# Two transformer stacks on one core: the plain blocks of the feed-forward's up projection go over to seven products, and attention scores are made two heads at a time

## The chip, the cores and the metric

The kernel runs on one core of a Trainium2 chip. TensorE (PE in the profile) multiplies matrices; VectorE (DVE) and ScalarE (ACT) work element by element; GpSimd (POOL) and SyncE (SP) mostly issue transfers. Each engine takes its instructions in the order in which the program lists them. The metric is the device time of one execution, 3244.63 us as the median of three runs (3244.62 to 3246.77). All arithmetic that matters is in single precision.

## The reference

512 tokens of width 1024 pass through four layers, each a mixer and then a feed-forward part, both added to x. Layers 1 and 2 mix with an mLSTM, an RG-LRU and a sparse attention (8 heads of width 64); their feed-forward has 3072 hidden columns. Layers 3 and 4 mix with a full attention and a memory attention; their feed-forward has 2816. What the change touches:

```
def rms_norm(x, g):
    return x * lax.rsqrt(jnp.mean(x * x, -1, keepdims=True) + EPS) * g

# feed-forward, layers 1 and 2
h = rms_norm(x, norm_ffn[l])
ff_g, ff_u = jnp.split(h @ ffn_up[l], 2, axis=-1)
ff_g = causal_dwconv(ff_g, ffn_conv_w[l], ffn_conv_b[l])
x = x + (jax.nn.gelu(ff_g) * ff_u) @ ffn_down[l]
# layers 3 and 4: x + (silu(gate) * up) @ w_down, without a convolution

# sparse attention, for each of 8 heads of width 64
att = einsum('bqhd,bqkhd->bqhk', q, k_sel) * Dh ** -0.5
p = softmax(where(keep, att, -inf)); y = einsum('bqhk,bqkhd->bqhd', p, v_sel)
```

The factor rsqrt(...) belongs to a token alone, so it may be applied to h @ W as well as to h.

## The kernel before

x is kept transposed, as eight tiles of 128 columns of the width by 512 tokens. A single-precision product is made of three products in a faster format (`three`, L436): every weight and every activation is split into a high and a low half, the high one by ACT (L361) and the low one by DVE (L369). So a weight chunk costs one `wh<-raw` and one `wl<-raw,wh` of 128x1024, and a matmul of the program shows as three of the trace.

The program is not written in the order in which it runs. Parts of it are generators; a list scheduler that runs when the kernel is built (`Issue`, L98) takes from them whatever its own table of durations and the priorities say is ready, and so fixes the order on each engine. Every engine then follows that order, ready or not. Temporaries are 66 slots of 128x512 and eight banks for results of TensorE; a part that finds too few slots waits for its turn.

**Norm.** `Norm.add(c)` (L919) runs when tile c of x is final: it makes the pair `hh`, `hl` of x g, and adds the squares to `nacc`. After the eighth, `finish` (L945) sums over the width on TensorE (`ps_st`), takes the root (`rn`, on POOL) and spreads it over the partitions (`ps_bc`): R, which is 1/rms for every token.

**Up projection.** `ffn` (L1890) goes through blocks of 256 gate columns and 256 up columns. The first two (`NOLD`) are *plain*: 192 matmuls of 512 columns in all, 96 a block, that read `hh` and `hl`, so that they can start before R is known; R is applied to their results. The other blocks use seven products in place of eight (a Strassen scheme): the inputs are cut into 2x2 quarters, and sums of quarters are multiplied, P1 to P7, each 24 matmuls of 256 columns. The weights' sums are formed by accumulating transfers. The sums of the activation's quarters (`xa`, `xb`, `xs`) are made by `Seven.build` (L1752) out of x g R, once, beside the plain blocks. P1 and P2 share a bank, so do P6 and P7, P5 and P3; P4 has its own. The order is a written list: P7 of the block before comes after P1, then P2, P5, the P4 and P3 of the block before, P6. Groups of two blocks are then multiplied down (`ps_t<-ff`), in units placed between the products.

**Sparse attention.** `dsa_head` (L1550) makes the scores of one head (`ps_at`), 20 matmul records on 64 of the 128 rows of the array; then DVE masks, ACT takes the exponent, DVE divides, PE transposes (`ps_pt`), ACT copies (`pT`), PE multiplies with v (`ps_y`). A head takes 12 slots. Two heads lie in one tile of q and of k, one in rows 0 to 63, the other in rows 64 to 127.

Of the kernel before, what the change touches and what calls it, by code (L numbers as in the profile page):

```python
# [17 lines left out]
P = 128  # L18
# [8 lines left out]
NOLD = 2  # L27
# [39 lines left out]
WIDTH = 4  # L67
ORDER = ("qi small mv av swap rx0 rx2 rg0 rg2 mk0 mk4 mk2 mk6 mo0 mo2 aq b0 b2 b6 ak b4 a0 a2 a4 a6 c0 c2 c4 c6",) * 2
# [261 lines left out]
def kernel(ctx, tc, a, out):  # L330
# [217 lines left out]
    behind, later = Chain(None, 0), Chain(None, 2)  # L548

    def after(fn, chain=behind):  # L550

        old, order.cur = order.cur, chain
        fn()
        order.cur = old
# [89 lines left out]
    def proj_t(w, c0, ntile, src, evac, ready=None, pre=None, ktiles=8, need=3):  # L644

        for i0 in range(0, ntile, 2):
# [433 lines left out]
    def first_mix(l, norm, nxt):  # L1080
# [454 lines left out]
        py, npv = {}, {}  # L1535
        nd = [0]

        def dsa_all():
            while len(masks) < NT or len(st["qcT"]) < NT or len(st["kcT"]) < NT or len(av) < NT:
                yield "wait"  # L1540
            for h in range(8):
                spawn(dsa_head(h), PRIO["dsa"])
                yield
                yield
# [5 lines left out]
        def dsa_head(h):  # L1550
            qc, kc = st["qcT"], st["kcT"]
            hp = h // 2
            rg = slice(64 * (h % 2), 64 * (h % 2) + 64)
            while len(slots.left) < 12:
                yield "wait"
            pr = [slots.take(F32, "pr") for _ in range(NT)]
            mx, nm, ssum = sm(4, "mx"), sm(4, "nm"), sm(4, "ss")
            where = {}

            def score(*tbs):  # L1560
                o = 0
                ps = yield from gbank("ps_at", 1)
                for tb in tbs:
                    for sb in range(tb + 1):
                        mm32(ps.t[:, o + sb * P:o + (sb + 1) * P], qc[tb].t[rg, hp * P:(hp + 1) * P],
                             kc[sb].t[rg, hp * P:(hp + 1) * P])
                    where[tb] = (ps, o)
                    o += (tb + 1) * P

            def top(t0, *tbs):  # L1570
                for tb in tbs:
                    ps, o = where[tb]
                    S = (tb + 1) * P
                    masked(pr[tb].t[:, 0:S], ps.t[:, o:o + S], masks[tb][:, 0:S], mx[:, tb:tb + 1])
                for ps in dict.fromkeys(where[tb][0] for tb in tbs):
                    ps.free()
                vts(nm[:, t0:t0 + len(tbs)], mx[:, t0:t0 + len(tbs)], -0.125, ALU.mult)

            def expo(*tbs):
                for tb in tbs:  # L1580
                    S = (tb + 1) * P
                    act(pr[tb].t[:, 0:S], pr[tb].t[:, 0:S], AF.Exp, scale=0.125, bias=nm[:, tb:tb + 1],
                        accum_out=ssum[:, tb:tb + 1])

            def norm_(t0, *tbs):
                recip(ssum[:, t0:t0 + len(tbs)], ssum[:, t0:t0 + len(tbs)])
                for tb in tbs:
                    S = (tb + 1) * P
                    vts(pr[tb].t[:, 0:S], pr[tb].t[:, 0:S], ssum[:, tb:tb + 1], ALU.mult)

            yield from score(0, 1)
            yield from score(2)
            yield
            top(0, 0, 1, 2)
            yield from score(3)
            yield
            expo(0, 1, 2)
            top(3, 3)
            yield
            norm_(0, 0, 1, 2)  # L1600
            expo(3)
            yield
            norm_(3, 3)
            yield
            pT = {}
            for grp in (((0, 0),), ((1, 0),), ((2, 0), (3, 256))):
                ps = yield from gbank("ps_pt", 1)
                for sb, o in grp:
                    tr(ps.t[:, o:], [pr[tb].t[:, sb * P:(sb + 1) * P] for tb in range(sb, NT)])
                if grp[0][0] == 0:  # L1610
                    ps0 = ps
                    continue
                if grp[0][0] == 1:
                    ps1 = ps
                    yield
                    for sb, p_ in ((0, ps0), (1, ps1)):
                        pT[sb] = (yield from grab("pT"))[0]
                        act(pT[sb].t[:, 0:T - sb * P], p_.t[:, 0:T - sb * P])
                        p_.free()
                    continue  # L1620
                yield
                b = (yield from grab("pT"))[0]
                act(b.t[:, 0:384], ps.t[:, 0:384])
                ps.free()
            for p_ in pr:
                p_.free()
            yield
            while hp not in py:
                if len(banks.left) > 2:
                    py[hp] = banks.take(F32, "ps_y")  # L1630
                else:
                    yield "wait"
            for sb in range(NT):
                N = T - sb * P
                v = b.t[:, (0 if sb == 2 else 256):][:, 0:N] if sb >= 2 else pT[sb].t[:, 0:N]
                mm32(py[hp].t[rg, sb * P:T], av[sb].t[:, h * 64:(h + 1) * 64], v, sb == 0, sb == NT - 1)
            for p_ in (pT[0], pT[1], b):
                p_.free()
            nd[0] += 1
            npv[hp] = npv.get(hp, 0) + 1  # L1640
            if npv[hp] == 2:
                p = yield from gpair("yc")
                split2(py[hp].t, p.h, p.l)
                py[hp].free()
                yc[hp] = p
            if nd[0] == 8:
# [93 lines left out]
        yield from proj_t(a["w_out"][l], 0, 8, lambda: [merged[i] for i in range(8)], ev_o, pre=pre_o, need=4)  # L1740
# [4 lines left out]
    class Seven:  # L1745
# [3 lines left out]
        def __init__(self):  # L1749
            self.v, self.bufs, self.done = {}, [], False  # L1750

        def build(self, norm):  # L1752
            yield from until(lambda: norm.R is not None)
            for k in range(KH):
                while len(slots.left) < 10:
                    yield "wait"
                t = [slots.take(F32, "hn") for _ in range(2)]
                for j in range(2):
                    stt(t[j].t[:, 0:T], xs[k + KH * j], cc(norm.g, k + KH * j), norm.R, ALU.mult, ALU.mult)
                a11, a21 = t[0].t[:, 0:256], t[0].t[:, 256:T]  # L1760
                a12, a22 = t[1].t[:, 0:256], t[1].t[:, 256:T]
                xa = slots.take(F32R, "xa")
                xb = pair("xb")
                splits([(a11, xa.t[:, 0:256], xa.t[:, 256:T]), (t[1].t[:, 0:T], xb.h, xb.l)])
                yield
                s = [slots.take(F32, "xs") for _ in range(2)]
                s1, s2, s3, s4 = s[0].t[:, 0:256], s[0].t[:, 256:T], s[1].t[:, 0:256], s[1].t[:, 256:T]
                vtt(s1, a21, a22, ALU.subtract)
                vtt(s2, s1, a11, ALU.subtract)
                vtt(s3, a11, a21, ALU.subtract)  # L1770
                vtt(s4, a12, s2, ALU.add)
                for b in t:
                    b.free()
                yield
                ps = [pair("xs") for _ in range(2)]
                splits([(s[j].t[:, 0:T], ps[j].h, ps[j].l) for j in range(2)])
                for b in s:
                    b.free()
                self.bufs += [xa, xb] + ps
                self.v[k] = dict(A11=(xa.t[:, 0:256], xa.t[:, 256:T]))  # L1780
                for nm, p, j in (("A12", xb, 0), ("A22", xb, 1), ("S1", ps[0], 0), ("S2", ps[0], 1),
                                 ("S3", ps[1], 0), ("S4", ps[1], 1)):
                    self.v[k][nm] = (p.h[:, j * 256:(j + 1) * 256], p.l[:, j * 256:(j + 1) * 256])
                yield
            self.done = True
# [4 lines left out]

    class Block:

        def __init__(self, X, w, cols, gate, done):
            self.X, self.gate, self.done = X, gate, done
# [19 lines left out]
        BANK = dict(P1="b1", P2="b1", P6="b2", P7="b2", P4="b3", P5="b4", P3="b4")  # L1816
        NEED = dict(P1=1, P2=2, P6=1, P7=2, P4=2, P5=0, P3=4)

        def mm(self, nm, x, h, lo):
            yield from until(lambda: self.X.done and len(slots.left) >= self.NEED[nm])  # L1820
# [5 lines left out]
            for j in range(2):  # L1826
                for k in range(KH):
# [3 lines left out]
                          not first and j == 1 and k == KH - 1, skip_group_check=True)  # L1831
# [9 lines left out]
        def after_P2(self):  # L1841
            self.g = [now(name="fg") for _ in range(2)]
            for j, v in enumerate(self.halves(self.b1)):
                self.gate.first(self.g[j].t[:, 0:256], v)
            self.b1.free()

# [3 lines left out]
        def after_P6(self):  # L1850
            self.u2 = now(name="u2")
            vtt(self.u2.t[:, 0:T], self.b2.t, self.s1.t[:, 0:T], ALU.add)

# [881 lines left out]
```

## Time and profile before

| | us |
|---|---|
| median of three runs | 3244.63 |
| the profiled execution, its own time | 3243.72 |
| its span | 3241.9 |
| PE busy | 3196.7 (99%) |
| DVE busy | 2201.1 (68%) |
| ACT busy | 1574.5 (49%) |

A matmul's modelled duration overlaps the next one's, so what one costs is read from one start to the next; so for DVE and ACT, whose rows overlap a little when they are queued without a wait. `[2.41 <-ACT s L361]` behind a row says that the engine sat idle for 2.41 us before it, until that instruction released it. A matmul that the program makes in single precision without the three products (`ps_at`, `ps_sc`, `ps_st`, `ps_bc`) shows as two records.

### The profile page before, as it was taken

The numbers are of one execution on the slowest core, as the hardware profiler recorded it, in microseconds if no ns is written. First come the engines' busy times: TensorE is split into PE (matmuls) and PEld (weight loads), VectorE is DVE, ScalarE is ACT, GpSimd is POOL, SyncE is SP. The second block draws the span as 40 slices with busy tenths as digits, with TensorE's granted clock in tenths as the row PEclk, the third lists the DMA queues.
The fourth block names the chain that finished last, engine by engine and source line by source line (L and its number), as shares of the span: only waits on it lengthen the run. The fifth ranks groups of instructions, "written<-read, shape, count | busy, mean of one in ns | idle before, by whom it ended". The sixth has DMA issues, their size and how long they took to land.

```text
span 3241.9 us, 45750 instructions
## 1 busy us (share of the span) xinstructions
PE 3196.7 (99%) x17637; PEld 2713.1 (84%) x17637; DVE 2201.1 (68%) x4154; ACT 1574.5 (49%) x2694; POOL 362.0 (11%) x407
## 2 busy tenths in 40 slices
PE   8999999999999999999999999999999999999999
PEld 6778778889987778778789988878899988889998
DVE  7974544766777974544766677787766667776664
ACT  6552433444444552433444456876443457664443
POOL 2000000011110000000011112120111111101110
PEclk9999999999999999999999999999999999999999
DMA  4323223377762323123377763221577742227783
GB/s 154 99 71 91 59 71 118 98 156 173 165 155 82 98 72 91 59 71 118 98 160 172 167 158 123 65 92 48 122 177 164 183 162 66 72 72 163 163 173 94
DMA packets 350345, 380.50 MB, mean 117 GB/s; under 512 B 17519, under 2 KB 324448, under 8 KB 350128
## 3 DMA queue, kind: packets, MB, share of 16 engines
q1 hardware_dynamic: 262256, 276.47, 27.5%
q0 software_dynamic: 87840, 101.12, 18.3%
q8 instruction: 138, 2.26, 0.3%
q14 instruction: 79, 0.65, 0.1%
q10 hardware_dynamic: 32, 0.01, 0.0%
HBM read 367.05 MB, written 10.49 MB: 116 GB/s over the span
## 4 chain that ended last, share of the span: by engine, by line
PE 90%; DVE 6%; issue 2%; ACT 1%; DMA 0%; POOL 0%; SPq 0%; DVEq 0%; POOLq 0%; ACTq 0%
PE ps_t L433 46%; PE ps_u L433 21%; PE ps_n L433 11%; PE ps_at L433 2%; PE ps_y L433 2%; PE ps_pt L425 2%; DVE wl L369 1%; PE ps_at L421 1%; PE ps_y L421 1%; DVE m L1238 1%; DVE score L1239 1%; ACT pr L361 1%; PE ps_num L421 1%; DVE u L369 1%; PE ps_S L421 1%
## 5 line engine op out<-in xcount | busy, mean ns | idle before, releaser
L369 DVE TENSOR_TENSOR wl<-raw,wh 128x1024 fp32r<-128x1024 f32 (+1 forms) x647 | 774.6, 1199 | 531.9 <-ACT wh L361 526.7
L361 ACT ACTIVATE wh<-raw 128x1024 fp32r<-128x1024 f32 (+1 forms) x647 | 672.1, 1040 | 944.0 <-PE ps_t L433 422.3
L433 PE MATMUL ps_u<-xsh,wl 128*128 128x256 f32 x1216 | 341.9, 281 | 3.1 <-DVE u L369 3.1
L433 PE MATMUL ps_u<-xsh,wh 128*128 128x256 f32 x1216 | 341.5, 281 | 0.0
L433 PE MATMUL ps_u<-xsl,wh 128*128 128x256 f32 x1216 | 341.1, 281 | 0.0
L433 PE MATMUL ps_t<-ffh,wl 128*128 128x512 f32 x736 | 290.3, 396 | 5.0 <-DVE wl L369 4.9
L433 PE MATMUL ps_t<-ffl,wh 128*128 128x512 f32 x736 | 290.2, 395 | 0.7 <-DVE ffl L369 0.7
L433 PE MATMUL ps_t<-ffh,wh 128*128 128x512 f32 x736 | 290.4, 395 | 0.0
L433 PE MATMUL ps_t<-h2h,wl 128*128 128x512 f32 x704 | 283.0, 402 | 0.0
L369 DVE TENSOR_TENSOR x<-x,ps_t 128x512 f32<-128x512 f32 x232 | 159.0, 686 | 182.7 <-PE ps_t L433 182.4
L433 PE MATMUL ps_t<-h2h,wh 128*128 128x512 f32 x704 | 282.8, 402 | 0.0
L433 PE MATMUL ps_t<-h2l,wh 128*128 128x512 f32 x704 | 280.0, 398 | 0.0
L433 PEld LDWEIGHTS ps_u<-xsh,wl 128*128 128x128 f32 x1216 | 229.1, 188 | 5.7 <-DVE u L369 4.0
L433 PEld LDWEIGHTS ps_u<-xsl,wh 128*128 128x128 f32 x1216 | 228.9, 188 | 1.7
L433 PEld LDWEIGHTS ps_u<-xsh,wh 128*128 128x128 f32 x1216 | 229.0, 188 | 0.0
L433 PE MATMUL ps_u<-xbh,wl 128*128 128x256 f32 x608 | 171.4, 282 | 6.4 <-ACT s L361 6.3
L433 PE MATMUL ps_u<-xbl,wh 128*128 128x256 f32 x608 | 171.2, 282 | 0.0
L433 PE MATMUL ps_u<-xbh,wh 128*128 128x256 f32 x608 | 171.1, 281 | 0.0
L433 PEld LDWEIGHTS ps_t<-ffh,wl 128*128 128x128 f32 x736 | 138.3, 188 | 37.1 <-DVE wl L369 8.1
L416 POOL DMA_DIRECT2D raw<-in_ffn_up_dram x80 | 102.3, 1366 | 564.5 <-DVE wl L369 508.4
L433 PEld LDWEIGHTS ps_t<-ffh,wh 128*128 128x128 f32 x736 | 138.2, 188 | 32.0
L433 PEld LDWEIGHTS ps_t<-ffl,wh 128*128 128x128 f32 x736 | 138.2, 188 | 30.3 <-DVE ffl L369 1.2
(454 smaller groups left out, 7268.3 us busy)
## 6 DMA issues: line engine op xcount, KB each, us to landing
raw<-in_w_in_dram SPq DMA_DIRECT2D x128, 512.0 KB, 3.8
raw<-in_ffn_up_dram SPq DMA_DIRECT2D x96, 512.0 KB, 4.7
raw<-in_w_gate_up_dram SPq DMA_DIRECT2D x88, 512.0 KB, 3.9
raw<-in_ffn_up_dram POOLq DMA_DIRECT2D x80, 512.0 KB, 5.9
raw<-in_w_gate_up_dram POOLq DMA_DIRECT2D x72, 512.0 KB, 6.0
raw<-in_w_out_dram SPq DMA_DIRECT2D x40, 512.0 KB, 3.5
raw<-in_ffn_down_dram SPq DMA_DIRECT2D x36, 512.0 KB, 4.4
raw<-in_w_down_dram SPq DMA_DIRECT2D x32, 512.0 KB, 5.1
```

What stands on the lines that cost most here:

```text
L361: lambda: nc.scalar.activation(out=out, in_=in_, func=func, **kw),
L369: dve(0.00104, lambda: nc.vector.tensor_tensor(out=out, in0=in0, in1=in1, op=op), [out], [in0, in1])
L416: order.op("pool", 1.0, lambda: nc.gpsimd.dma_start(out=out, in_=in_, accum_op=ALU.add), [out], [out], extra=max(n, 0.05), slack=-1.0)
L421: lambda: nc.tensor.matmul(o, lhsT=lhsT, rhs=rhs, start=start, stop=stop), [o], [lhsT, rhs],
L425: order.op("pe", 0.107, lambda: nc.tensor.transpose(o, in_, idn), [o], [in_, idn], rows=in_.shape[0])
L433: lambda: nc.tensor.matmul(o, lhsT=lhsT, rhs=rhs, start=first, stop=last, **kw), [o], [lhsT, rhs],
L1238: dve(0.00104, lambda: nc.vector.max(out=m8, in_=acc), [m8], [acc])
L1239: dve(0.00104, lambda: nc.vector.match_replace(out=acc, in_to_replace=m8, in_values=acc, imm_value=MARK), [acc], [acc, m8])
```

## The change

- **Norm.** A `NormSeven` replaces the norm ahead of each feed-forward part: it makes no `hh`, `hl`, but from x g the quarters and their sums, tile by tile as x comes out of the mixer's output projection. That projection takes its tiles in the order 0 and 1, 4 and 5, 2 and 3, 6 and 7 (`TURNS`), since tiles k and k+4 are summed together.
- **Up projection.** All blocks go by seven products. R is applied to results, on DVE. P7 has a bank of its own. The first two blocks are interleaved by a written list.
- **Scores.** Heads go in pairs; the two heads' products stand alternately in the queue, in two banks; a pair takes 16 slots.

```diff
-NOLD = 2
+TURNS = (0, 4, 2, 6)
...
-        def dsa_head(h):
-            while len(slots.left) < 12:
+        def dsa_pair(hp):
+            while len(slots.left) < 16:
                 yield "wait"
...
                     for sb in range(tb + 1):
-                        mm32(ps.t[:, o + sb * P:o + (sb + 1) * P], qc[tb].t[rg, hp * P:(hp + 1) * P],
-                             kc[sb].t[rg, hp * P:(hp + 1) * P])
+                        for j, rg in enumerate(rgs):
+                            mm32(pss[j].t[:, o + sb * P:o + (sb + 1) * P], qc[tb].t[rg, hp * P:(hp + 1) * P],
+                                 kc[sb].t[rg, hp * P:(hp + 1) * P])
...
+    class NormSeven(Norm):
+        def add(self, c):
+            t = self.t[c] = now(name="xg")
+            act(t.t[:, 0:T], xs[c], scale=cc(self.g, c))
+            self.X.own(c, t)
+            k = c % KH
+            if k in self.t and k + KH in self.t:
+                spawn(self.X.sums(k, [self.t[k], self.t[k + KH]]), 0)
+            self.acc = self.sq(c, self.acc)
...
-        BANK = dict(P1="b1", P2="b1", P6="b2", P7="b2", P4="b3", P5="b4", P3="b4")
+        BANK = dict(P1="b1", P2="b1", P6="b2", P7="b7", P4="b3", P5="b4", P3="b4")
...
         def after_P2(self):
             self.g = [now(name="fg") for _ in range(2)]
+            spawn(self.first(), 0)
+
+        def first(self):
+            yield from until(self.norm.ready)
             for j, v in enumerate(self.halves(self.b1)):
-                self.gate.first(self.g[j].t[:, 0:256], v)
+                vtt(self.g[j].t[:, 0:256], v, self.norm.R[:, 0:256], ALU.mult)
...
         def gates(self):
+            R = self.norm.R
             for j in range(2):
-                self.g[j] = self.gate.rest(j, self.g[j])
+                v = self.g[j].t[:, 256:T]
+                vtt(v, v, R[:, 256:T], ALU.mult)
+            for j in range(2):
+                self.g[j] = self.gate(j, self.g[j])
+                v = self.g[j].t[:, 0:T]
+                vtt(v, v, R, ALU.mult)
...
-        for b in range(nblk):
-            if b < NOLD:
-                yield from plain(b, fs)
-                continue
...
+        for b, nm in ((0, "P1"), (0, "P2"), (1, "P1"), (1, "P2"), (0, "P5"), (0, "P7"), (1, "P5"), (0, "P6"), (1, "P7"),
+                      (0, "P3"), (1, "P6"), (0, "P4"), (2, "P1"), (1, "P3"), (2, "P2"), (1, "P4"), (2, "P5")):
+            yield B[b].u[nm]
+        yield from between(2, "P5")
```

**First place: PE at the third feed-forward part.** The queue of before, from some way into the first plain block (`hh`, `hl`: the norm's pair; `wh`, `wl`: a weight's halves):

```order
L433 MATMUL ps_t<-hh,wl 128x512
L433 MATMUL ps_t<-hl,wh 128x512
L421 MATMUL ps_st<-ones,nacc 128x1 x4
L433 MATMUL ps_t<-hh,wh 128x512
L433 MATMUL ps_t<-hh,wl 128x512
L433 MATMUL ps_t<-hl,wh 128x512
L433 MATMUL ps_t<-hh,wh 128x512
L433 MATMUL ps_t<-hh,wl 128x512
L433 MATMUL ps_t<-hl,wh 128x512
L433 MATMUL ps_t<-hh,wh 128x512
L421 MATMUL ps_bc<-ident,rn_20714 128x128 x4
```

The queue of the change at the same place, from the end of the output projection (`yoh`, `yol`) into P1 of block 0 (`ps_u<-xa`):

```order
L433 MATMUL ps_t<-yoh,wl 128x512
L433 MATMUL ps_t<-yol,wh 128x512
L433 MATMUL ps_t<-yoh,wh 128x512
L421 MATMUL ps_st<-ones,nacc 128x1 x4
L421 MATMUL ps_bc<-ident,rn_21224 128x128 x4
L433 MATMUL ps_u<-xa,wl 128x256
L433 MATMUL ps_u<-xa,wh 128x256 x2
L433 MATMUL ps_u<-xa,wl 128x256
```

Before, `ps_st` and `ps_bc` stand among plain matmuls; now they stand straight behind the projection and ahead of the first product. The fourth part has the same rows. In the first two, `ps_st` and `ps_bc` stand inside P2 of block 0.

**Second place: DVE behind P4 of block 1 in the first feed-forward part.** The queue of the change; `fg` is the gate, `fy` its convolution, R_5032 the 1/rms, `ff` what the down projection reads. In PE's queue P4 of block 1 is followed by P5 of block 2 (24 matmuls) and by the first down unit, whose first 12 matmuls read block 0's `ff` and whose next 12 read block 1's:

```order
L369 TENSOR_TENSOR fg<-fg,R_5032 128x256
L373 SCALAR_TENSOR_TENSOR fy<-fg,colt_98,fy 128x511
L373 SCALAR_TENSOR_TENSOR fy<-fg,colt_97,fy 128x510
L373 SCALAR_TENSOR_TENSOR fy<-fg,colt_98,fy 128x511
L369 TENSOR_TENSOR wl<-raw,wh 128x1024
L369 TENSOR_TENSOR fy<-fy,R_5032 128x512
L369 TENSOR_TENSOR wl<-raw,wh 128x1024
L373 SCALAR_TENSOR_TENSOR fy<-fg,colt_97,fy 128x510
L369 TENSOR_TENSOR u<-u,fy 128x512
L369 TENSOR_TENSOR fy<-fy,R_5032 128x512
L369 TENSOR_TENSOR ffl<-u,ffh 128x512
```

Ahead of these rows, since P4's end, stand three more of 128x256 and six of 128x512. Before, block 1 was plain, and its `ff` was made while P1 to P5 of block 2 ran.

**Third place: PE in the sparse attention of the first layer.** One head of before, from its transposes on (`h2h`, `h2l` and `ps_t`: another projection's matmuls):

```order
L425 MATMUL ps_pt<-ident,pr 128x128 x10
L433 MATMUL ps_t<-h2h,wl 128x512
L433 MATMUL ps_t<-h2l,wh 128x512
L433 MATMUL ps_t<-h2h,wh 128x512
L421 MATMUL ps_y<-pT,av 64x512
L421 MATMUL ps_y<-pT,av 64x384
L421 MATMUL ps_y<-pT,av 64x256
L421 MATMUL ps_y<-pT,av 64x128
L421 MATMUL ps_at<-rT 128x128 x10
```

The third pair of the change, with scores of the fourth:

```order
L425 MATMUL ps_pt<-ident,pr 128x128 x10
L421 MATMUL ps_at<-rT 128x128 x6
L421 MATMUL ps_y<-pT,av 64x512
L421 MATMUL ps_y<-pT,av 64x384
L421 MATMUL ps_y<-pT,av 64x256
L421 MATMUL ps_y<-pT,av 64x128
L421 MATMUL ps_at<-rT 128x128 x6
L425 MATMUL ps_pt<-ident,pr 128x128 x10
L421 MATMUL ps_at<-rT 128x128 x8
L421 MATMUL ps_y<-pT,av 64x512
```

Scores, transposes and products with v of two pairs now follow one another with no other projection's matmul between them, and the last pair ends shortly before its result is read; before, single heads were spread among other work, and the last ended some 220 matmuls earlier.

## Rows read from the trace of the kernel before

**Rows 1.** The page, busy time, share and instructions by engine.
```profile
PE 3196.7 (99%) x17637; PEld 2713.1 (84%) x17637; DVE 2201.1 (68%) x4154; ACT 1574.5 (49%) x2694; POOL 362.0 (11%) x407
```
**Rows 2.** The page, the chain that ended last, by engine.
```profile
PE 90%; DVE 6%; issue 2%; ACT 1%; DMA 0%; POOL 0%; SPq 0%; DVEq 0%; POOLq 0%; ACTq 0%
```
**Rows 3.** PE's waits: line, who was waited for, total us, times, longest.
```profile
PE ps_t L433 <- DVE wl L369: 7.5, 16, 1.3
PE ps_u L433 <- ACT s L361: 6.3, 4, 2.4
...
PE ps_u L433 <- DVE u L369: 3.1, 4, 0.8
```
**Rows 4.** PE's timeline, first feed-forward part's head: start, us, engine, line, operation.
```profile
597.42 0.40 PE L433 MATMUL ps_t<-hh,wl 128*128 128x512 f32 x1
...
604.11 1.05 PE L421 MATMUL ps_bc<-ident,rn 128*128 128x128 f32 x8
...
645.36 0.28 PE L433 MATMUL ps_u<-xa,wl 128*128 128x256 f32 x1
...
647.94 0.40 PE L433 MATMUL ps_u<-xa,wh 128*128 128x256 f32 x2
650.75 0.39 PE L433 MATMUL ps_u<-xbh,wl 128*128 128x256 f32 x1 [2.41 <-ACT s L361]
```
**Rows 5.** PE's timeline, third feed-forward part's head.
```profile
2270.20 0.39 PE L433 MATMUL ps_t<-hh,wl 128*128 128x512 f32 x1
...
2277.36 1.05 PE L421 MATMUL ps_bc<-ident,rn 128*128 128x128 f32 x8
...
2316.60 0.28 PE L433 MATMUL ps_u<-xa,wl 128*128 128x256 f32 x1
...
2320.36 0.39 PE L433 MATMUL ps_u<-xbh,wl 128*128 128x256 f32 x1 [0.75 <-ACT s L361]
```
**Rows 6.** Windows after the heads of parts one and two: PE busy, PEclk, DMA.
```profile
645.00:660.00 15.00, 12.59 (x84) 0.89 0.51 112
...
1617.00:1632.00 15.00, 12.59 (x90) 1.00 0.55 119
```
**Rows 7.** PE, groups of tile ps_at: instructions, ns min/median/max, first and last start.
```profile
L421 PE MATMUL ps_at<-rT x320: 272/272/373, 356.8 to 1409.4; 64*128 64x128 f32 x160
```
**Rows 8.** PE's timeline, score products on 64 rows: ps_at of one head, ps_sc.
```profile
356.79 2.50 PE L421 MATMUL ps_at<-rT 64*128 64x128 f32 x20
...
59.47 1.34 PE L421 MATMUL ps_sc<-kiT,rT 64*128 64x256 f32 x4
...
78.15 1.78 PE L421 MATMUL ps_sc<-kiT,rT 64*128 64x384 f32 x8
...
81.00 1.12 PE L421 MATMUL ps_sc<-kiT,rT 64*128 64x512 f32 x2
```
**Rows 9.** DVE's timeline, end of the third layer's output projection.
```profile
2266.10 0.68 DVE L369 TENSOR_TENSOR nacc<-nacc,sq 128x512 f32<-128x512 f32 x1
2266.70 0.74 DVE L373 SCALAR_TENSOR_TENSOR hl<-x,colt,hh 128x512 fp32r<-128x512 f32 x1
2267.37 0.68 DVE L369 TENSOR_TENSOR nacc<-nacc,sq 128x512 f32<-128x512 f32 x1
...
2268.57 1.22 DVE L369 TENSOR_TENSOR wl<-raw,wh 128x1024 fp32r<-128x1024 f32 x1
2269.70 0.74 DVE L373 SCALAR_TENSOR_TENSOR hl<-x,colt,hh 128x512 fp32r<-128x512 f32 x1
...
2281.15 0.42 DVE L369 TENSOR_TENSOR xa<-hn,xa 128x256 fp32r<-128x256 f32 x1
2281.48 0.68 DVE L369 TENSOR_TENSOR xbl<-hn,xbh 128x512 fp32r<-128x512 f32 x1
```
**Rows 10.** DVE's timeline, last block of the first feed-forward part.
```profile
958.52 0.41 DVE L369 TENSOR_TENSOR fg<-ps_u,s 128x256 f32<-128x256 f32 x1
...
969.31 1.28 DVE L369 TENSOR_TENSOR ffl<-u,ffh 128x512 fp32r<-128x512 f32 x2
```

More of the change, by code (lines that the diff above doesn't have):

```diff
@@ L546, in split, with after @@
         u.w = (h, lo, hv, lv)
-    behind, later = Chain(None, 0), Chain(None, 2)
-    def after(fn, chain=behind):
-        old, order.cur = order.cur, chain
+    behind = Chain(None, 0)
+    def after(fn):
+        old, order.cur = order.cur, behind
         fn()
@@ L1625, in dsa_head @@
[L1625 to L1636, printed above, removed]
@@ L1637, in dsa_head @@
-            for p_ in (pT[0], pT[1], b):
-                p_.free()
-            nd[0] += 1
[L1640 to L1646, printed above, removed]
+            for j, rg in enumerate(rgs):
+                pT = {}
+                for grp in (((0, 0),), ((1, 0),), ((2, 0), (3, 256))):
+                    ps = yield from gbank("ps_pt", 1)
+                    for sb, o in grp:
+                        tr(ps.t[:, o:], [pr[j][tb].t[:, sb * P:(sb + 1) * P] for tb in range(sb, NT)])
+                    if grp[0][0] == 0:
+                        ps0 = ps
+                        continue
+                    if grp[0][0] == 1:
+                        ps1 = ps
+                        yield
+                        for sb, p_ in ((0, ps0), (1, ps1)):
+                            pT[sb] = (yield from grab("pT"))[0]
+                            act(pT[sb].t[:, 0:T - sb * P], p_.t[:, 0:T - sb * P])
+                            p_.free()
+                        continue
+                    yield
+                    b = (yield from grab("pT"))[0]
+                    act(b.t[:, 0:384], ps.t[:, 0:384])
+                    ps.free()
+                for p_ in pr[j]:
+                    p_.free()
+                yield
+                if j == 0:
+                    while len(banks.left) <= 2:
+                        yield "wait"
+                    py = banks.take(F32, "ps_y")
+                for sb in range(NT):
+                    N = T - sb * P
+                    v = b.t[:, (0 if sb == 2 else 256):][:, 0:N] if sb >= 2 else pT[sb].t[:, 0:N]
+                    h = 2 * hp + j
+                    mm32(py.t[rg, sb * P:T], av[sb].t[:, h * 64:(h + 1) * 64], v, sb == 0, sb == NT - 1)
+                for p_ in (pT[0], pT[1], b):
+                    p_.free()
+                yield
@@ L1738, in ev_o @@
                     p.free()
-        yield from proj_t(a["w_out"][l], 0, 8, lambda: [merged[i] for i in range(8)], ev_o, pre=pre_o, need=4)
+        yield from proj_t(a["w_out"][l], 0, 8, lambda: [merged[i] for i in range(8)], ev_o, pre=pre_o, need=4, turns=TURNS)
     KH = 4
@@ L1749, in __init__ @@
         def __init__(self):
[L1750 to L1761, printed above, removed]
+            self.v, self.bufs = {}, []
@@ L1762, in build, with own @@
+        def own(self, c, t):
+            v = self.v.setdefault(c % KH, {})
+            if c < KH:
                 xa = slots.take(F32R, "xa")
+                self.bufs.append(xa)
+                v["A11"] = xa.t[:, 0:256], xa.t[:, 256:T]
+                split2(t.t[:, 0:256], *v["A11"])
+            else:
                 xb = pair("xb")
-                splits([(a11, xa.t[:, 0:256], xa.t[:, 256:T]), (t[1].t[:, 0:T], xb.h, xb.l)])
-                yield
-                s = [slots.take(F32, "xs") for _ in range(2)]
@@ L1777, in build @@
[L1777 to L1785, printed above, removed]
+                self.bufs.append(xb)
@@ L1866, in after_P4 @@
             self.s1.free()
-            after(self.gates, later)
+            spawn(self.gates(), 2)
         def gates(self):
+            while self.state < 1 or len(slots.left) < 2:
+                yield "wait"
+            R = self.norm.R
             for j in range(2):
-                self.g[j] = self.gate.rest(j, self.g[j])
+                v = self.g[j].t[:, 256:T]
+                vtt(v, v, R[:, 256:T], ALU.mult)
+            for j in range(2):
+                self.g[j] = self.gate(j, self.g[j])
+                v = self.g[j].t[:, 0:T]
+                vtt(v, v, R, ALU.mult)
+            self.state = 2
         def after_P3(self):
@@ L1877, in after_P3 @@
             self.u2.free()
-            after(self.ends, later)
+            spawn(self.ends(), 2)
         def ends(self):
+            while self.state < 2 or len(slots.left) < 4:
+                yield "wait"
             for j in range(2):
@@ L1945, in ffn @@
         nblk = k0 // 2
-        places = [(b, nm) for b in range(NOLD, nblk) for nm in ("P1", "P5")] + [(nblk, "P4"), (nblk, "end")]
+        places = [(b, nm) for b in range(2, nblk) for nm in ("P1", "P5")] + [(nblk, "P4"), (nblk, "end")]
         last = max(ends)
@@ L1951, in ffn @@
         done = sorted(ends)
-        first = [places.index((max(NOLD, e + 2), "P1")) if e + 2 < nblk else len(places) - 2 for e in done[:-1]]
+        first = [places.index((max(2, e + 2), "P1")) if e + 2 < nblk else len(places) - 2 for e in done[:-1]]
         first[0] = 1
```

248 lines of the change are left out of this document (116 added, 132 removed).

## Prediction

> **What bounds the kernel now.** I read the busy shares first: PE is busy for 99% of the span, DVE for 68%, ACT for 49% [rows 1]. The chain that ended last agrees: 90% of it is PE, 6% DVE [rows 2]. So time goes where matmuls go, or where a new wait stops PE. Third I read PE's waits: there are few. 6.3 us in four waits belong to the switch from plain blocks to products, 3.1 us in four to the bank that P6 and P7 share; the wait for a weight's low half, 7.5 us in sixteen, is spread over the program [rows 3]. Fourth, the timelines of the places that the change touches. The reader should see that PE has no slack to give: what the change saves on PE is saved at once, and each new wait of PE costs its full length.
>
> **What it removes.**
>
> *Plain blocks.* In the first feed-forward part they run from 597.42 to 645.36, 47.94 us [rows 4]; in the third from 2270.20 to 2316.60, 46.40 us [rows 5]. Parts two and four have the same 192 matmuls, so I take them like one and three: 188.7 us in all. To this belong the waits behind P1, 6.3 us [rows 3], and one fall of the clock: after 2.41 us of idleness PE got a granted clock of 0.89 over 15 us and did 84 records; after the same idleness in part two it kept 1.00 and did 90 in the same busy time [rows 6]. Six records fewer, counted as 512-column matmuls of 0.233 us, (46.40 - 1.6) / 192 by rows 5, are 1.4 us. Sum: 196.4 us.
>
> In their place come 14 products of 24 matmuls. P1 shows 22 starts from 645.36 to 647.94, 0.117 us each [rows 4]; 14 x 24 x 0.117 is 39.3 us, and the 16 records of `ps_st` and `ps_bc`, of which eight last 1.05 us [rows 4], add 1.6. Four parts: 4 x 40.9 = 163.8. **Saved: 32.6 us.**
>
> *Scores.* 320 records on 64 of the array's rows [rows 7]. One head's 20 take 2.50 us, the last of them 0.27 long [rows 7, 8], so (2.50 - 0.27) / 19 = 0.117 us from one to the next, 37.5 us together. Does it help to alternate halves of the array? The trace has no `ps_at` in that order, but `ps_sc` in both: two records of 512 columns alone take 1.12 us, while eight of 384 columns and more, heads of both halves side by side, take 1.78 [rows 8]. That is 0.56 against 0.22 us a record, and more than half is gone. Bounds: nothing saved, or half of 37.5, 18.8. I take 17, nearest to the `ps_sc` rows. The Trainium skill, TensorEngine Tiling (Array Packing), Key Properties, says that tiles of the array work independently and that a change of the tiling drains the engine; the rows agree with the first, and by the second, pairs would change it less often than heads and save a little more than 17. **Saved: 17 us.**
>
> *P7's own bank.* The 3.1 us of P6 and P7 [rows 3] go. **Saved: 3.1 us.** Together 52.7.
>
> **What it adds.** DVE queues at these distances: 0.60 us for 128x512 (2266.10 to 2266.70), 0.67 with a scalar, 1.13 for `wl`, 0.33 for 128x256 [rows 9].
>
> *Heads of parts three and four.* PE's queue now has `ps_st` and `ps_bc` between the projection and P1 (first place). The row of before tells how long that chain is: the first plain matmul, straight behind the projection, starts at 2270.20, `ps_bc` at 2277.36, 7.16 us later [rows 5], hidden by plain matmuls. Now nothing hides it. 0.8 us of it is `ps_st` itself, leaving 6.4; `ps_st` may have stood 0.8 us in its queue, leaving 5.6; but DVE has three more instructions ahead of the last sum, and five ahead of `msq`, some 2.5 us. Bounds 5.6 and 8.5; I take 7.0. Two parts: 14 us. Behind P1 on PE all of the block waits; nothing else is ready there.
>
> *Heads of parts one and two.* `ps_st` stands within P2, 31 matmuls or 3.6 us behind the projection, and its chain to the last sum is a little longer: 1 us each (0 to 2.5), 2 us.
>
> *First down unit, parts one and two* (second place). From P4's end to the high half of block 1's `ff` DVE makes four of 128x256, eight of 128x512, four with a scalar and two `wl`: 1.32 + 4.8 + 2.68 + 2.26 = 11.1 us, with 0.4 to see P4's end and 0.6 for ACT's half 12.1. Before, the same chain without R took 10.8 us in the last block, 958.52 to 969.31 [rows 10]. What covers it: P5 of block 2, 2.8 us, and twelve matmuls of 512 columns, 2.8 us. Idle: 12.1 - 5.6 = 6.5 (bounds 4 and 9). Two parts: 13 us. *Parts three and four* have no convolution; the same count gives about 7.6 against 5.6: 2 us each, 4 us.
>
> *Last block of part one.* R lengthens the chain of rows 10 by four of 0.33 and two of 0.60: 2.5 us. In part two the last group is of six tiles, which covers it.
>
> *Score stage* (third place). Between `ps_pt` and `ps_y` ACT copies three tiles; where other matmuls stood now a few scores stand, an estimated 0.5 to 1 us too few, four times a layer. 2.5 us a layer, 5 us (0 to 16).
>
> *Clock.* PE now idles 6.5 to 7 us at four places. One of two idle times of 2.41 us was followed by a lower clock [rows 6]; these are longer, so I count 1.4 us at each, 5.6 us (bounds 0 and 8). The Trainium skill, TensorE: Matmul & The Clock Gate, HAM oscillation, states that idle gaps of PE throttle it again after each; it speaks against this change, and 0.89 in one window of two agrees half.
>
> DVE's rest: 46 blocks with eight more products by R less the old ones and 24 more `wl` are some 80 us of DVE in 3240, 68% becoming 71%: hidden by PE, except in the chains above. Transfers that accumulate (32 more on POOL) are for blocks 0 and 1, issued during the mixer: nothing.
>
> Added: 14 + 2 + 13 + 4 + 2.5 + 5 + 5.6 = 46.1 us. Net -52.7 + 46.1 = **-6.6 us** against the profiled execution's 3243.72; that lies 0.9 below the median 3244.63, so the forecast is 3244.6 - 6.6 = 3238 us.
>
> **The rivals.**
>
> *The waits are smaller than counted.* For it: DVE is idle for 32% [rows 1], so its queue may be empty where I let it be full, and `ps_st` may lose less. If the heads cost 5.6, the down units 4, the scores nothing and the clock nothing: 11.2 + 8 + 2 + 2.5 = 24 us instead of 46, 3216 us. Against it: the 7.16 us of rows 5 are measured.
>
> *DVE's longer chain makes every down unit late* (the slower side). In parts one and two each block's `ff` comes 2.5 us later; 22 further blocks have a down unit whose distance was fitted to the chain of before, 10.8 us [rows 10]. It decides where the cover behind P4 is under some 13 us; 1.1 us a block would give 24 us, 3262 us. For it: the chain of rows 10 was already waited for. Against: these units stand two products later than the first one.
>
> *Scores don't overlap.* Had `ps_at`, with 128 columns a record, too little to run side by side, the 17 us stay: 3255 us. Against: rows 8.
>
> *No clock falls:* 3232 us, part of the forecast's own range.
>
> **How the numbers follow.** Forecast, 3228 to 3248: 0.48. Smaller waits: 0.23. Late down units: 0.18. Scores apart: 0.08; 0.03 for others. About 0.2%, 6.5 us, is what a measurement can tell from no change: 3238.1 to 3251.1. The forecast's case lies half below it: 0.24 faster, 0.22 same, 0.02 slower. With 0.23 faster, and 0.26 and 0.03 mostly slower: 0.47 faster, 0.24 same, 0.29 slower. The range runs from the first rival to the second, 3213 to 3263; with both signs in it, the forecast's own is 3228 to 3248.
>
> **What would show it.** In the new profile: PE idle for about 7 us between the third projection and P1, released by DVE's `wl` or by `ps_bc`; about 6.5 us ahead of the first `ps_t<-ff` in part one, released by ACT's `ffh`; a lower PEclk just after each; no wait of P7 for P6; `ps_at` in half its time; parts one to four each about 7 us shorter from the end of the projection to the end of the second block. Wrong if these waits are under 3 us, if `ps_at` takes as long as before, or if DVE's releases of `ps_t<-ff` recur in every block.

## The result, and the profile after

The changed kernel takes 3270.11 us (median of four runs, 3269.48 to 3272.97), 25.5 us more than the 3244.62 of the kernel before in the same comparison; the ratio is 1.0085 [1.0069, 1.0100]. The forecast was 3238, its range ended at 3263, so the sign and the range were missed.

The page of the changed kernel, busy time, share and instructions by engine:

```profile
PE 3177.6 (97%) x18213; PEld 2718.4 (83%) x18213; DVE 2308.9 (71%) x4454; ACT 1590.5 (49%) x2650; POOL 413.4 (13%) x439
```

PE is busy 19 us less than before [rows 1], as its matmuls are fewer in columns, and the span is 26.5 us longer: PE waits. A measure of the waits: for every PE record the distance to the next start, less the median distance for its line, tile and shape, summed. Before, that is 73.7 us, now 126.7. The measure misleads for the score products alone: they now start in pairs, two at nearly the same time, so that a median step says little. Their 320 starts took 40.0 us before and 20.6 now. With these set apart, the other matmuls' usual steps fell by 19.5 us, so PE's work fell by 39 us in all, and its lost time rose from 69.6 to 134.7, by 65. PE's waits of the changed kernel (line, who was waited for, total us, times, longest):

```profile
PE ps_t L433 <- ACT ffh L361: 17.5, 11, 5.3
PE ps_bc L421 <- POOL rn L398: 13.5, 3, 6.9
PE ps_t L433 <- DVE wl L369: 11.5, 15, 2.1
PE ps_st L421 <- DVE nacc L369: 9.6, 3, 4.5
PE ps_u L433 <- ACT s L361: 7.3, 8, 1.6
...
PE ps_u L433 <- DVE u L369: 1.9, 4, 0.5
```

Against [rows 3]: the waits for `ffh`, for `rn` and for `nacc` are new (or nearly: the longest of them before was 0.5 us), the one behind P1 (`<- ACT s`) has not gone but come at eight places in place of four, and P6's and P7's (`<- DVE u`) is smaller, not gone. PE's timeline at the head of part three (start, us, operation, idle time before it and who ended it), the place of [rows 5]:

```profile
2271.85 0.40 PE L433 MATMUL ps_t<-yoh,wh 128*128 128x512 f32 x1
2276.71 1.17 PE L421 MATMUL ps_st<-ones,nacc 128*128 128x1 f32 x8 [4.46 <-DVE nacc L369]
2284.82 2.08 PE L421 MATMUL ps_bc<-ident,rn 128*128 128x128 f32 x8 [6.95 <-POOL rn L398]
2286.55 0.56 PE L433 MATMUL ps_u<-xa,wl 128*128 128x256 f32 x1
```

From the projection's last matmul to P1 14.7 us pass. The 6.95 us wait is for one small instruction of GpSimd. GpSimd at that place, first in the changed kernel, then in the one before:

```profile
2279.02 5.75 POOL L398 TENSOR_TENSOR rn<-msq,mhalf 128x4 f32<-128x4 f32 x1 [51.29 <-DVE msq L379]
```
```profile
2276.07 1.01 POOL L398 TENSOR_TENSOR rn<-msq,mhalf 128x4 f32<-128x4 f32 x1 [77.87 <-DVE msq L379]
```

The same 128x4 takes 5.75 us in place of 1.01. What DVE did meanwhile, in the changed kernel:

```profile
2278.78 0.15 DVE L379 TENSOR_SCALAR msq<-ps_st 128x4 f32<-128x4 f32 x1
2278.85 1.21 DVE L369 TENSOR_TENSOR wl<-raw,wh 128x1024 fp32r<-128x1024 f32 x1
2279.99 0.42 DVE L369 TENSOR_TENSOR xs<-xg,xs 128x256 f32<-128x256 f32 x1
2280.32 0.68 DVE L369 TENSOR_TENSOR xsl<-xs,xsh 128x512 fp32r<-128x512 f32 x1
2280.92 1.22 DVE L369 TENSOR_TENSOR wl<-raw,wh 128x1024 fp32r<-128x1024 f32 x1
2282.06 0.68 DVE L369 TENSOR_TENSOR xsl<-xs,xsh 128x512 fp32r<-128x512 f32 x1
2282.66 1.22 DVE L369 TENSOR_TENSOR wl<-raw,wh 128x1024 fp32r<-128x1024 f32 x1
```

Six instructions without a gap, each of two tensors in SBUF, until 2283.88; the root ends 0.9 us later, at 2284.77, about its usual length. Before, DVE was idle there. Part four shows the same: 5.68 us, ended 0.9 us behind DVE's last. The Trainium skill, SBUF — State Buffer, SBUF: two separate sides, says that VectorE and GpSimd share a pair of ports as an exclusive lock, that an instruction of VectorE with two SBUF inputs takes it against one of GpSimd that reads SBUF, and that the loser blocks. The rows agree in the length, and show more than a single instruction's: both times GpSimd's ended only behind the last of VectorE's row. That the ports are the reason is the page's account; the rows don't separate it from another.

PE at the first down unit of part one:

```profile
646.66 0.73 PE L433 MATMUL ps_t<-ffh,wl 128*128 128x512 f32 x2 [1.09 <-ACT ffh L361]
...
649.73 0.40 PE L433 MATMUL ps_t<-ffh,wh 128*128 128x512 f32 x1
655.38 1.22 PE L433 MATMUL ps_t<-ffh,wl 128*128 128x512 f32 x2 [5.25 <-ACT ffh L361]
```

Twelve matmuls on block 0, then the wait for block 1, as forecast: 1.1 + 5.3 us, and 0.9 in smaller gaps. Windows of the changed kernel in the four parts (PE busy, PEclk, DMA share, GB/s), and one of the kernel before:

```profile
595.00:601.50 6.50, 6.50 (x32) 0.50 0.80 164
653.00:659.50 6.50, 4.12 (x10) 0.50 0.99 148
974.00:976.80 2.80, 2.80 (x7) 0.50 0.63 187
1626.00:1632.20 6.20, 4.53 (x11) 0.50 1.11 168
2278.00:2287.50 9.50, 2.68 (x12) 0.50 0.25 66
2902.50:2915.50 13.00, 6.75 (x31) 0.50 0.38 78
```
```profile
652.20:655.40 3.20, 3.20 (x16) 0.50 0.86 197
```

PEclk 0.50 is the lower of the granted clock's two levels, 1.2 GHz in place of 2.4. In these windows, 44.5 us together, the changed kernel ran at it, each time during or behind a wait of PE; the kernel before did so for 3.2 us of its four parts. And the scores, where [rows 8] had 20 records in 2.50 us:

```profile
369.06 2.50 PE L421 MATMUL ps_at<-rT 64*128 64x128 f32 x40
```

Forty records in the time of twenty.

### The profile page after: what moved, and what is told of

Its sections match the earlier page's. It is cut to its first block, busy times and chain, and to the rows that moved or that the text cites. A ratio compares the mean times of both kernels' runs of the same rounds, so it can differ in the third digit from the quotient of the medians.

```text
span 3268.4 us, 47241 instructions
## 1 busy us (share of the span) xinstructions
PE 3177.6 (97%) x18213; PEld 2718.4 (83%) x18213; DVE 2308.9 (71%) x4454; ACT 1590.5 (49%) x2650; POOL 413.4 (13%) x439
## 5 line engine op out<-in xcount | busy, mean ns | idle before, releaser
L361 ACT ACTIVATE wh<-raw 128x1024 fp32r<-128x1024 f32 (+2 forms) x671 | 697.5, 1040 | 1000.4 <-PE ps_t L433 382.0
L369 DVE TENSOR_TENSOR wl<-raw,wh 128x1024 fp32r<-128x1024 f32 (+2 forms) x671 | 804.9, 1200 | 513.6 <-ACT wh L361 511.8
L433 PE MATMUL ps_u<-xsh,wl 128*128 128x256 f32 x1472 | 414.1, 281 | 1.9 <-DVE u L369 1.9
L433 PE MATMUL ps_u<-xsl,wh 128*128 128x256 f32 x1472 | 413.3, 281 | 0.0
L433 PE MATMUL ps_u<-xsh,wh 128*128 128x256 f32 x1472 | 413.1, 281 | 0.0
L433 PE MATMUL ps_t<-ffh,wl 128*128 128x512 f32 x736 | 291.5, 401 | 29.1 <-ACT ffh L361 17.5
L433 PEld LDWEIGHTS ps_u<-xsh,wl 128*128 128x128 f32 x1472 | 277.1, 188 | 4.4 <-DVE u L369 2.7
L433 PEld LDWEIGHTS ps_u<-xsl,wh 128*128 128x128 f32 x1472 | 277.2, 188 | 1.7
L433 PEld LDWEIGHTS ps_u<-xsh,wh 128*128 128x128 f32 x1472 | 277.1, 188 | 0.0
L433 PE MATMUL ps_u<-xbh,wl 128*128 128x256 f32 x736 | 208.1, 283 | 8.8 <-ACT s L361 7.3
L416 POOL DMA_DIRECT2D raw<-in_w_gate_up_dram x88 | 112.6, 1363 | 566.3 <-DVE wl L369 459.7
```

Source lines behind the costliest of these rows:

```text
L361: lambda: nc.scalar.activation(out=out, in_=in_, func=func, **kw),
L369: dve(0.00104, lambda: nc.vector.tensor_tensor(out=out, in0=in0, in1=in1, op=op), [out], [in0, in1])
L416: order.op("pool", 1.0, lambda: nc.gpsimd.dma_start(out=out, in_=in_, accum_op=ALU.add), [out], [out], extra=max(n, 0.05), slack=-1.0)
L433: lambda: nc.tensor.matmul(o, lhsT=lhsT, rhs=rhs, start=first, stop=last, **kw), [o], [lhsT, rhs],
```

## The experiments

Every run was compared with the kernel before on the same chip, whose median was 3242.0 us for the first four, then 3244.0 for the next four, 3244.6 for three and 3243.8 for the last. Where times of two chips are subtracted below, the chips themselves differ by up to 2.6 us: each taken against its own kernel before, the 17.6, 11.2, 16.7, 7.9, 6.1 and 26.5 us below become 20.2, 8.6, 14.1, 9.8, 4.1 and 25.9. No conclusion hangs on the difference.

**Pairs alone.** The kernel before, with the changed kernel's `dsa_pair` in place of `dsa_head`.

> The kernel before with one edit: scores of two heads at a time; the feed-forward is as it was. Theory A (the pairs save what was forecast, and the loss is all in the feed-forward): about 17 us less than before, 3224 to 3230 us, ps_at in about half its time. Rival B (a pair's 16 slots and its crowded transposes eat the saving): no change, 3240 to 3248 us.

Measured: 3226.53, ratio 0.9951 [0.9939, 0.9964], 15.5 us less. In its trace the 320 score products' starts take 20.6 us, as in the changed kernel. Theory A holds.

**Single heads.** The changed kernel, with `dsa_head` in place of `dsa_pair`.

> The changed kernel with one edit: scores by single heads again. Theory A: about 18 us more than the changed kernel's 3270, 3284 to 3292 us. Rival B (pairs hold slots and banks that the rest needs): 3270 us or less.

Measured: 3287.70, 17.6 over the changed kernel. With the run above: the pairs are worth 16 to 20 us in either setting, so the rest of the change costs 41 to 46.

**The root on DVE.**

```diff
-            rsqrt(rn, m)
+            order.op("pool", 0.96, lambda: nc.vector.reciprocal(out=rn, in_=m), [rn], [m])
```

> The changed kernel, in which GpSimd's root ahead of each feed-forward part is left out: a reciprocal on VectorE (1/x in place of x^-0.5) takes its place in the same order. In the changed kernel GpSimd's root took 5.7 us in parts three and four while VectorE ran without a gap, and 1.0 before. Theory C (GpSimd is held up by VectorE, and PE waits for it): ps_bc starts 4.6 us earlier in parts three and four, with the clock 9 to 12 us in all, 3258 to 3261 us. Rival D (VectorE's queue is the cause, and the wait moves to P1's wl): 0 to 3 us, 3267 to 3270 us.

Measured: 3258.95, 11.2 less. PE at the head of part three, and DVE's instruction:

```profile
2273.04 1.87 PE L421 MATMUL ps_st<-ones,nacc 128*128 128x1 f32 x8 [4.46 <-DVE nacc L369]
2276.54 2.08 PE L421 MATMUL ps_bc<-ident,rn 128*128 128x128 f32 x8 [1.63 <-DVE rn L956]
```
```profile
2276.32 0.17 DVE L956 RECIPROCAL rn<-msq 128x4 f32<-128x4 f32 x1
```

The order is the same, the wait 1.63 in place of 6.95 us. Theory C holds; D would have kept the time. By the traces 9.6 us of the gain lie ahead of P1 in parts three and four, and 3.1 in part one, where the window of the lower clock at 595 us is missing in this run.

**The sums later.**

```diff
-                spawn(self.X.sums(k, [self.t[k], self.t[k + KH]]), 0)
+                spawn(self.X.sums(k, [self.t[k], self.t[k + KH]]), 3)
```

> The changed kernel with one number changed, the priority at which the sums of quarters are issued (0 to 3), so that P1's weights are split before them and P1 and part of P2 stand ahead of ps_st on PE in parts three and four. Theory E (the two waits of PE between projection and P1, 12 us each with GpSimd's root inside them, cost their full length): 20 to 27 us less with the clock, 3243 to 3250 us. Rival F (VectorE has the same work to do, and the wait comes back at P2 or at the first use of a sum): under 10 us less, 3260 to 3268 us.

Measured: 3253.38, 16.7 less, between the two. PE at the head of part three:

```profile
2271.28 0.39 PE L433 MATMUL ps_t<-yoh,wh 128*128 128x512 f32 x1
2271.51 0.28 PE L433 MATMUL ps_u<-xa,wl 128*128 128x256 f32 x1
...
2275.34 0.39 PE L433 MATMUL ps_u<-xbh,wl 128*128 128x256 f32 x1 [0.84 <-ACT s L361]
2276.04 1.02 PE L421 MATMUL ps_st<-ones,nacc 128*128 128x1 f32 x8
```

P1 starts straight behind the projection. The wait ahead of P2 stood there before (0.69 us, now 0.84). What came back: 1.2 us at `ps_bc` and 2.2 at the first products that read late sums, in each of the two parts. So both theories are partly right: the two waits were long because nothing stood behind them that could run, and some 3.5 us of each 12 came back.

**P1, P1, P2, P2** (with the sums later).

```diff
-        for b, nm in ((0, "P1"), (0, "P2"), (1, "P1"), (1, "P2"), (0, "P5"), (0, "P7"), (1, "P5"), (0, "P6"), (1, "P7"),
+        for b, nm in ((0, "P1"), (1, "P1"), (0, "P2"), (1, "P2"), (0, "P5"), (0, "P7"), (1, "P5"), (0, "P6"), (1, "P7"),
```

> The kernel with the sums issued later, and the first two blocks' list begun with P1 of block 0, P1 of block 1, then the two P2, in place of P1, P2, P1, P2. Theory G (P2 adds to P1's bank and waits there for ScalarE's copy of P1, 0.85 to 1.2 us at each of eight places): 6 to 9 us less than the run with the sums later (3253 us), 3244 to 3248 us. Rival H (P2 waits for operands that come at the same time anyway): 0 to 2 us, 3251 to 3254 us.

Measured: 3245.53, 7.9 less than with the sums later, ratio to before 1.0007 [0.9999, 1.0016]. Theory G has the size: P2 adds to the bank of P1 and must wait until ACT has copied P1 out of it. PE's waits now (the head of the list, without `ps_u <- ACT s`):

```profile
PE ps_t L433 <- ACT ffh L361: 17.4, 11, 5.3
PE ps_t L433 <- DVE wl L369: 11.3, 15, 1.9
PE ps_u L433 <- ACT xsh L361: 5.8, 2, 2.9
```

The last row was 1.3 us with the sums later, and its two waits lie in parts three and four. From their first product to their last down unit these two parts got only 0.3 us shorter each, parts one and two 3.3 each. So G holds in parts one and two; in three and four PE waits for late sums instead, as rival H had it.

**The first down unit later** (with the sums later, list as in the change).

```diff
-        first[0] = 1
+        first[0] = 3
```

> The kernel with the sums issued later, and the first down unit moved from behind P5 of block 2 to behind P5 of block 3, six products later (17 us of cover more). Theory I (PE's 7.3 us wait in parts one and two and 2.0 us in three and four are the chain of VectorE alone): these go, 18.6 us, and the lower clock behind the two long ones, 3 to 4 us: 3230 to 3236 us. Rival J (the units stand closer now and wait there for weights or slots): half of it comes back, 3241 to 3250 us.

Measured: 3259.45, 6.1 more. (In the queue the unit moved by five products, 120 matmuls, some 14 us.) Both theories fall. PE's waits, and DVE's busy time in the window of part one's head:

```profile
PE ps_u L433 <- DVE wl L369: 21.0, 10, 4.6
...
PE ps_t L433 <- ACT ffh L361: 4.7, 7, 3.0
```
```profile
632.00:647.00 15.00, 14.33 (x24) 0.91 0.66 153
```

The wait for `ffh` went from 17 to 5 us, and 21 us for weights' low halves came: without a down unit there PE asks for the next product's weights sooner, and DVE, busy 14.3 of 15 us, makes either `ff` or `wl`. The changed kernel itself has the same stretch, 13.5 of 15 us:

```profile
634.00:649.00 15.00, 13.54 (x24) 1.00 0.84 201
```

In this order it is DVE's work in that stretch that is too much, not the place of one wait; my forecast had treated it as a chain with a cover. The parts differ: against the run with the sums later one and two got 3.2 and 1.2 us shorter, three and four 5.1 and 3.2 longer. Whether it helps to split weights ahead, in the stretch before (602 to 617 us, where DVE was busy for 7.8 of 15), was not run.

**No R on the gates.** The changed kernel without four of a block's six products by R; 1/rms is left out there.

```diff
-                vtt(v, v, R[:, 256:T], ALU.mult)
+                pass
...
-                vtt(v, v, R, ALU.mult)
+                pass
```

> The changed kernel without the four products by R on the gate's second half and behind the gate (1/rms is left out there; the two behind P1 and P2 stay), 1.86 us of VectorE a block. Theory K (R's products lengthen the chain that the down units wait for): the first down wait of 7.3 us falls by about 3 us in parts one and two, the recurring waits of part one and the last wait of one and two by another 3 each: 12 to 16 us less than 3270, 3254 to 3258 us. Rival L (the chain is the convolution and the weights' halves; R's products run in gaps): under 5 us less, 3265 to 3270 us.

Measured: 3243.61, 26.5 less, twice what theory K had. PE's waits for the down units:

```profile
PE ps_t L433 <- DVE wl L369: 6.9, 14, 2.4
PE ps_t L433 <- DVE ffl L369: 1.5, 3, 0.6
PE ps_t L433 <- ACT ffh L361: 1.4, 2, 0.7
```

17.5 us for `ffh` became 1.4, 11.5 for `wl` 6.9; the lower clock behind these waits went too. The order of PE's products is the same in both traces, so the gain can be placed. Up to the end of the first down unit it is 7.3, 7.4, 2.0 and 2.2 us in the four parts, 18.8 together; in the products behind it 8.2, of which 4.9 in part one; in the down units behind the last product 3.5. (These are 30.5; some 4 us came back between the parts.)

**Pairs and P7's bank.** Pairs alone, with P7's own bank as in the change.

> The kernel before with the scores in pairs and with P7's own bank, nothing else of the change. Theory A with the forecast's third saving: 3 to 4 us less than pairs alone (3226.5 us, 15.5 below its kernel before), so 18 to 20 us below the kernel before, 3222 to 3226 us. Rival: a bank more makes another part wait, no gain over pairs alone.

Measured: 3228.68, 15.3 below its kernel before, ratio 0.9958 [0.9944, 0.9971], against 15.5 for pairs alone. No gain of the bank's 3.1 us is seen, though the two intervals are too wide to rule it out. In the trace of this run the waits for `u` are gone, and others for `wl` are there that pairs alone doesn't have: 1.3 us at products and 2.4 in the last down group.

**R in the old blocks.** Pairs alone, with the four products by R put into the blocks that go by products, on top of an R already applied.

```diff
+                v = self.g[j].t[:, 256:T]
+                vtt(v, v, R[:, 256:T], ALU.mult)
...
+                v = self.g[j].t[:, 0:T]
+                vtt(v, v, R, ALU.mult)
```

> The kernel before with the scores in pairs, and in its product blocks (the third on) the same four products by R on VectorE that the change has on the gate's second half and behind the gate, here on top of an R already applied; the two plain blocks stay. They tell the steady blocks from the head. Theory N (VectorE is short only at the head of a part, where 14 products stand without a down unit): 3 to 8 us over pairs alone, about 0.25 at each down unit of parts one and two and 2 to 3 us at their ends: 3230 to 3236 us on a chip where the kernel before takes 3244. Rival K2 (the chain is too long in every block): 15 to 25 us over pairs alone, 3242 to 3253 us.

Measured: 3238.34, ratio 0.9983 [0.9974, 0.9991], so 10 us over pairs alone (0.32% of 3244), between the two. The down units of part one wait for `wl` 0.80 us each in place of 0.51, and every second one 0.46 more: in steady blocks too DVE is late by a little. All of it lies in parts one and two; three and four, which have no convolution, keep their length within 0.3 us. It is near the 8.2 us that the run without R won in the products behind the first down units.

**R on GpSimd** (with the sums later and P1, P1, P2, P2).

```diff
-                vtt(v, v, R, ALU.mult)
+                pool(1.3, lambda v=v: nc.gpsimd.tensor_tensor(out=v, in0=v, in1=R, op=ALU.mult), [v], [v, R])
```

> The kernel with the sums later and P1, P1, P2, P2 (3245.5 us), with the product by R behind the gate on GpSimd in place of VectorE, 1.2 us of VectorE a block less. Theory K (VectorE's work at the head is what PE waits for): 5 to 12 us less, 3233 to 3240 us. Rival O (GpSimd's 128x512 product is held up by VectorE's queue as its root was, 1.0 to 5.7 us, and comes later than VectorE's own): 10 us or more over it, above 3255 us.

Measured: 3267.64, 22.1 more. Rival O's time, though not its reason in full. GpSimd's groups (count, busy us, mean ns), and PE's waits:

```profile
L1928 POOL TENSOR_TENSOR fy<-fy,R 128x512 f32<-128x512 f32 x48 | 83.4, 1741 | 131.9 <-ACT fy L361 131.9
```
```profile
PE ps_t L433 <- ACT ffh L361: 18.4, 7, 6.1
PE ps_t L433 <- DVE ffl L369: 13.1, 17, 1.4
```

One product takes 1.74 us (the shortest 1.27) where DVE takes 0.60, and the down units wait for what follows it. How much of the 1.74 is DVE's holding the port was not separated.

**Products without R** (sums later, P1, P1, P2, P2, no R on the gates; 1/rms is left out there).

> The kernel with the sums later and P1, P1, P2, P2, and without the four products by R on the gate and behind it (1/rms is left out there). It tells what all blocks by products would be worth if R cost nothing. Theory P (26.5 us as in the changed kernel, the two repairs and R add up): 3217 to 3222 us, under pairs alone (16 us below the kernel before, 3228 us where that takes 3244). Rival Q (with the heads repaired the same stretch waits for weights): 3230 us or more.

Measured: 3217.85, 27.7 under the same with R. Theory P holds: all blocks by products would win 11 us over pairs alone if R were free (26.7 below the kernel before, against 15.5), and with R they lose 17 (1.5 above it).

**Pairs, and P5 behind the first P1.**

```diff
-            yield B.u["P2"]
-            yield B.u["P5"]
+            for nm in ("P2", "P5") if prev else ("P5", "P2"):
+                yield B.u[nm]
```

> A candidate beyond both kernels: the kernel before with the scores in pairs, and with P5 put between P1 and P2 in the first product block of each part (in the later blocks P7 of the block before stands there already). Theory G again (P2 waits for ScalarE's copy out of the bank that it shares with P1, 6.3 us over the four parts): 4 to 7 us under pairs alone, which lay 16 us below the kernel before: 3219 to 3224 us where that takes 3244. Rival (the product behind P1 waits there in any case, for operands or weights): no gain over pairs alone, 3226 to 3230 us.

Measured: 3219.24, ratio 0.9927 [0.9914, 0.9941], 24.5 us under the kernel before and 51 under the changed one: the fastest version with all of the computation in it. The wait `ps_u <- ACT s`, 6.3 us in [rows 3], is out of PE's list; two waits for `xsl`, 2.9 us in all, are new in parts one and two. The head of the list is now

```profile
PE ps_t L433 <- DVE wl L369: 7.3, 15, 1.4
PE ps_rg L421 <- DVE rx L373: 4.8, 4, 2.0
```

## Why the prediction was wrong

The forecast was 52.7 us saved and 46.1 added. The table sets its terms beside the two traces: the steps between PE's starts, beyond the usual step, sorted by place, the changed kernel less the one before. Of the 32.6 us that the forecast saved on plain blocks about 20 were matmuls and 12.6 waits of the old heads, the 6.3 behind P1 among them.

| term | forecast, us | in the traces, us |
|---|---|---|
| matmuls of plain blocks and scores | -37 | -39 |
| wait behind P1 | -6.3 | +1.6 |
| other waits of the old heads, their fall of the clock with them | -6.3 | -4.5 |
| waits of P6 and P7 for their bank | -3.1 | -1.3 |
| heads of the parts | +16 | +23.9 |
| first down units | +17 | +18.6 |
| last blocks | +2.5 | +6.0 |
| later down units, products waiting for `wl` | 0 | +5.9 |
| clock | +5.6 | +12.0 |
| steps under 0.25 us too long, at full clock | 0 | +4.6 |
| outside the four parts (score stage among it) | +5 | -1.8 |
| sum | -6.6 | +26 |

So the work on PE was forecast rightly, and no single wait makes the error: several steps failed, most of them in the same direction. The largest are the wait behind P1, the heads with GpSimd's root, the clock, and DVE's work called hidden.

- *Wait behind P1:* failed. I counted it as gone with the plain blocks, though it belongs to P1 and P2 standing together, and the change's list has that twice a part: 7.3 us in eight waits now. Undoing it gave 7.9 us, and in the kernel before, with pairs, another 7.3.
- *Heads of parts three and four, 14 us:* right in kind, the size was off: 4.5 and 7.0 us of idle time in part three, 22 in both parts. The step took GpSimd's root at the 1.0 us that it had in the chain of [rows 5], where DVE was idle. With a full queue on DVE it was 5.7. This is 11.2 us with the clock. The profile before held the warning only in DVE's idle time beside `rn`.
- *First down unit, 13 and 4 us:* right in size, 18.6 in all; in part one 6.3 us in two waits against 6.5. But the step's idea, a chain with a cover, was only half of it: moving the unit moved the wait to `wl`.
- *"DVE's rest ... hidden by PE, except in the chains above":* failed. R's four products on the gates cost 26.5 us of time; 18.8 of what they cost lie at the first down units, where the forecast had counted a chain with R in it, but 8.2 lie in the products behind, which it had at nothing, and 3.5 in the last down units, which it had at 2.5 for part one alone. DVE's mean of 71% hid that it has 13.5 of 15 us to do at the head of part one, where 17 products stand without a down unit, newly split weights are needed every 2.8 us, and two blocks' ends fall together. The slower rival had this mechanism, with a chance of 0.18, but put 24 us on the steady blocks.
- *Last block of part one, 2.5 us:* 3.7 in part one, and 2.3 in part two, where nothing was forecast. R isn't the cause of the second: without it 2.9 us stay, and the run with pairs and P7's bank alone has 2.9 there too.
- *Clock, 5.6 us:* too small. PE's starts at the lower clock lost 12.0 us over their usual steps, 1.5 before. The price of a fall had been read from a single one, and in parts three and four the waits ahead of it were longer than forecast.
- *P7's own bank, 3.1 us:* PE's wait went down by 1.3, and in the run with the bank alone the time did not fall.
- *Scores, 17 us:* right, 19.3 by the starts. Of the 5 us for a crowded score stage little is seen: the pairs gave 15.5 and 17.6 us where 12 net was forecast. (Outside the four parts the lost time lies between 34 and 47 us in the different runs, so the table's last row says little.)

Two smaller things: 4 x 40.9 is 163.6, not 163.8, which changes nothing; and the 0.4 us to see P4's end in the first down unit's sum has no row of its own.

That the sign was wrong follows: PE's work fell by 39 us as forecast, and the waits added were 65 us net, where the forecast's 46.1 less the 15.7 that it let go were 30.

## What to carry to other kernels

An engine's busy share over the whole span says nothing of a stretch in which two stages' ends meet: sum its work against the window in which it must be done. Where it filled the window here, 14.3 of 15 us, moving a wait only renamed it. A wait belongs to the two instructions that stand together (here a bank filled by one product and added to by the next), so look for them in the new order too, before counting the wait as saved. And a duration of GpSimd taken beside an idle VectorE, 1.01 us, did not hold beside a busy one, 5.75.

## What the runs showed of the hardware that was not expected

- GpSimd's 128x4 power took 5.75 and 5.68 us beside six VectorE instructions of two SBUF inputs in a row, 1.95 in parts one and two, and 1.01 beside none in the third part of the kernel before.
- Score products of 64 rows, alternating between the two halves of the array, ran in half the time in full: 40 records in 2.50 us against 20, and all 320 in 20.6 us by their starts against 40.0.
- A 128x512 product took GpSimd 1.74 us on average (48 of them, the shortest 1.27), against 0.60 from one to the next on VectorE.
